# Layer 0's mixer weights: low parts kept in DRAM between the pass over ctx and the pass over x

## The chip, the cores and the metric

One core of one Trainium2 chip runs the whole program. The metric is the device time of one execution in microseconds (us); a time is the median of several runs. The engines are TensorE (PE; its weight loads are PEld), VectorE (DVE), ScalarE (ACT), GpSimd (POOL) and SyncE (SP), which here does nothing but issue DMA transfers. Each engine runs its own instructions in the order of the program and waits where a result or a buffer is not there yet.

## What is computed

Two transformer blocks in float32, on 256 tokens of 1024 features. The first block works on x alone. The second has two layers (`DEPTH_2 = 2`) and two streams, x and ctx, of 256 tokens each. In layer 0 both streams go through the same mixer with the same weights, ctx first, since x attends to the keys, values and states that ctx leaves:

```python
for l in range(DEPTH_2):
    ...
    if last:
        mem = _context_memory(hc, p)
    else:
        yc, mem = _context_mixer(hc, p)
        ...
    x = _post(x, _latent_mixer(_modulate(x, sh1, sc1), mem, cos, sin, p), g1, ln1_g[l], ln1_b[l])
    x = _post(x, _ffn(_modulate(x, sh2, sc2), p), g2, ln2_g[l], ln2_b[l])

def _latent_mixer(h, mem, cos, sin, p):
    proj = h @ p['w_in']
    ...                                   # attention, gated linear attention, convolution of 31 taps
    return _merge(o_att, o_gla, r, glu, gates, p)    # three branches, gated, then w_out
```

In layer 1 the ctx stream needs only its keys, values and states, so only a part of the weights is used twice there.

## The kernel before

**Weights.** All weights come as *units* of 128 x 1024 float32 (512 KB), in the order in which they are used; `program` is run once with a stand-in to record that order (`self.order`), and then again to write the instructions. A product of float32 quality is made of three passes in the faster float32r form: `mm3` multiplies the weight's high part `whi` with the high part of the input, `whi` with the input's low part, and the weight's low part `wlo` with the input's high part. Each pass is 8 products of 128 x 256, so a unit is 24.

**The stream** (`unit` and `load`). When unit n is asked for, `unit` has SP issue the loads of the `raw` tiles up to unit n + 4 (5 `raw` buffers), and `load` splits the units up to n + 2: ACT copies `raw` into `whi` (which rounds it), then DVE or POOL subtracts, `wlo = raw - whi` (3 buffers each). Both instructions of the split stand under `high_priority(offset=75)`. A new `raw` load needs the buffer of five units before, which both instructions of the split must have read; a new `wlo` needs the third pass of the unit three before.

**Who subtracts.** `lo_eng` gives a share of the subtractions to POOL and the rest to DVE by counting them: 3 of 5 in layer 0's mixers (phase `m0t` in `LO`), 1 of 2 in the feed-forwards after them (`f0t`), none in the last one (`f1t`). The count also covers the splits of the branches' outputs (`yl`).

**The mixer** (`mix`) takes one stream through 109 units: keys, values, gates, queries, the convolution's input (`glu`), three branches with their gates (`gb0` to `gb2`, 48 units) and `out` (8 units). In its first part the attention's steps, the gated linear attention's (tiles `gF`, `cum`, `ga`) and the convolution's are woven with the products; the convolution is 248 DVE instructions per stream into the tile `ca`, at low priority (`offset=-1000`). The last two branches and `out` are nearly all products. The program calls `mix` for ctx and then for x.

**Order.** The order of each engine's instructions is made when the kernel is built: a scheduler takes what is written in `program` and moves instructions by their priority. On the chip the order is fixed. SP's queue is such an order too: a transfer that waits holds all that are issued behind it.

Of the kernel before, what the change touches and what calls it, by code (L numbers as in the profile page):

```python
# [18 lines left out]
P = 128  # L19
D = 1024  # L20
T = 256
# [6 lines left out]
# column ranges of the first block's w_in  # L28
# [6 lines left out]
# column ranges of the second block's w_in  # L35
# [11 lines left out]
def _plan():  # L47
    """Order of the weight units: (name, kind, count)."""
    p = [("memk", "F", 8), ("memv", "V", 8), ("lrux", "F", 8), ("lrug", "F", 8),
         ("foxq", "F", 8), ("foxk", "F", 8), ("foxv", "V", 8),  # L50
         ("sbq", "F", 8), ("sbk", "F", 8), ("sbv", "V", 8), ("memq", "F", 8)]
    p += [(f"gb{n}", "F", 16) for n in range(4)]
    p += [("out", "F", 8), ("gu", "F", 2 * FT), ("dn", "D", 24)]
    for l in range(2):
        p += [(f"k{l}", "F", 2), (f"v{l}", "V", 2), (f"kg{l}", "F", 4), (f"vg{l}", "V", 8), (f"glr{l}", "F", 1),
              (f"q{l}", "F", 8), (f"qg{l}", "F", 4), (f"r{l}", "F", 8), (f"glu{l}", "F", 16)]
        p += [(f"gb{n}_{l}", "F", 16) for n in range(3)]
        p += [(f"out{l}", "F", 8), (f"gu{l}", "F", 2 * FT), (f"dn{l}", "D", 24)]
    pos, o = {}, 0
    for name, _, n in p:  # L60
        pos[name] = o
        o += n
    return pos, o
# [4 lines left out]
# columns of the parameter array  # L68
# [18 lines left out]
# those of the first block alone  # L87
# [42 lines left out]
def _pack(x):  # L130
    """Lays the inputs out as the kernel streams them."""
# [160 lines left out]
def weave(*parts):  # L292
    """Interleaves generators: parts are (generator, steps per turn)."""
    live = list(parts)
    while live:
        live = [(g, n) for g, n in live if step(g, n)]


# the share of the weights whose low part GpSimd works out, the vector engine the rest
# [3 lines left out]
class Null:  # L303
    """Stands in for the chip while the order of the weight units is recorded."""
# [17 lines left out]
class Builder:  # L322
    AHEAD = 2

    def __init__(self, tc, a, ctx, order=None):
# [4 lines left out]
        # weight units: their order if known, what is loaded, what is used  # L330
# [13 lines left out]
        # brings in the scalar engine's table for the first norms  # L344
        warm = cp.tile([P, 1], F32, tag="warm", name="warm")
        self.act(warm, self.eps, AF.Sqrt)
        self.mmp = ep(name="mmp", bufs=3, space=bass.MemoryType.PSUM)
# [44 lines left out]
    def phase(self, name, t1=6, t2=6, t4=0):  # L392
        """Opens the pool of the short-lived tiles of a phase: 1, 2 and 4 KB rings."""
# [30 lines left out]
    def unit(self, idx, n=1024):  # L424
        """The next unit of the stream, split; loads run ahead of the use."""
# [10 lines left out]
        while self.n_ready < min(len(self.asked) + self.AHEAD, len(self.order)):  # L436
            self.ready.append(self.load(*self.raws.pop(0)))
# [3 lines left out]
    def load(self, raw, n):  # L441
        hi = self.wp.tile([P, 1024], F32R, tag="whi", name="whi", bufs=3)
        lo = self.wp.tile([P, 1024], F32R, tag="wlo", name="wlo", bufs=3)
        with self.tc.high_priority(offset=75):
            self.split(raw[:, :n], hi[:, :n], lo[:, :n])
        return hi, lo

    def mm3(self, o, w, x, nk, xk, first=True, last=True):
        """o (+)= w.T @ x over nk contraction tiles, in three float32r passes."""
# [10 lines left out]
    def pair(self, name, i, h, n=2):  # L460
        """Feature-major projection onto n feature tiles, from unit i on: [P, n * T] in PSUM."""
# [7 lines left out]
    def half(self, name, i, h, ps=None):  # L469
        """Unit i of a projection, into the first half of a new bank, or the second half of ps."""  # L470
# [8 lines left out]
    def proj_pair(self, name, ft, h):  # L479
        """Two feature tiles from paired units, [P, T] each in PSUM."""  # L480
# [4 lines left out]
    def tok(self, name, c, h):  # L485
        """Token-major projection onto 256 columns: [P, token tile, 256] in PSUM."""
# [13 lines left out]
    def rsqrt(self, ps, w, n):  # L500
        """1/sqrt(ps / n + EPS) on [P, w]."""
# [10 lines left out]
    def token_rsqrt(self, sq, nd, n):  # L512
        """1/sqrt(mean square + EPS) by token, from the squares of heads of nd tiles of features each, [P, T]:
        a column for each head and token tile."""
# [12 lines left out]
    def root(self, ps, w, n):  # L527
        """1/sqrt(ps / n + EPS) by way of the scalar engine."""
# [5 lines left out]
    def total(self, x, fast):  # L534
        """Sum over the features, on every partition; fast: in the fewest steps after the last feature."""
# [37 lines left out]
    def ln_core(self, x, xc, fast=False):  # L573
        """Centres x into xc; returns 1/std."""
# [9 lines left out]
    def post(self, z, g, b, fast=False):  # L584
        """LayerNorm of z with gain and bias, in place; steps: the norm's factor, then one per feature tile."""
# [13 lines left out]
    def attend(self, q, qr, segs, vt, nd, evac):  # L599
        """q: list of [P(d), T] chunks, without the norm's factor, which is qr (a column for each query tile);  # L600
        segs: lists of [P(d), T] key chunks; vt(kt, d): [P(key), P] values."""
# [35 lines left out]
    # ================= first block ======================================  # L637
# [86 lines left out]
    def halve(self, acc, mx):  # L724
        """Splits acc / 2."""
# [4 lines left out]
    def gated_all(self, name, h, y, acc, first, bias):  # L730
        """Steps, one per feature tile: twice sigmoid(gate) * (y @ w) is added to acc. The first two gates come
        ahead of the products of y, which may still be on its way."""
# [42 lines left out]
    def mem_norm(self, ps, out, g):  # L775
        """RMS norm of a head of 256 features (two feature tiles)."""
# [10 lines left out]
    def lru(self, h, y, bp):  # L787
        nc = self.nc
        for f in range(0, KT, 2):
# [13 lines left out]
            # gelu (tanh form) without its factor 1/2  # L803
# [11 lines left out]
    def lru_pair(self, f, xc, ga, y):  # L815
        nc = self.nc
        # nl = -log a = (tanh + 1) * (4 softplus(-lam)); ix = (tanh + 1) * xc = 2 i xc
# [13 lines left out]
        # -expm1(2 log a) = tanh(-log a) * (1 + a^2)  # L831
# [7 lines left out]
        # the scan and ga each carry a factor 2  # L839
# [4 lines left out]
    def fox(self, h, y, bp):  # L844
        nc = self.nc
        # forget gates: cumulative -log sigmoid, [16 heads, T]
# [11 lines left out]
        # -log_sigmoid(z) = ln(1 + exp(-|z|)) - min(z, 0)  # L858
# [19 lines left out]
        # the row that carries -cum_f of the key: where the other head's features are  # L878
# [19 lines left out]
    def fox_head(self, q, k, cm, rows):  # L898
# [4 lines left out]
        # negated masked logits and their minimum  # L903
# [17 lines left out]
    def softplus_abs(self, out, z):  # L921
        """ln(1 + exp(-|z|))"""
# [4 lines left out]
    def av_pair(self, y, ft, v, j, pts):  # L927
        """Two heads' values, side by side in the columns of the array."""
# [28 lines left out]
    def stick_pair(self, y, ft, v, j, qs, k, bp):  # L957
        """Two heads: those of one feature tile."""
# [4 lines left out]
        for half, q in enumerate(qs):  # L963
            z = self.ps("z")
            self.mm(z[:, :T], k[:, :P], q)
            # the bank's first product clears its accumulation bits, so this one overwrites and later ones add
# [5 lines left out]
        # softplus(z), only where key < query  # L972
# [5 lines left out]
        # z minus the suffix sums over keys  # L978
# [14 lines left out]
    # ================= feed-forward =====================================  # L993
    def ffn(self, gu, dn, h, hidden, down, bp):
        """Steps: one per hidden tile, then one per pair of output tiles."""
# [24 lines left out]
    # ================= second block =====================================  # L1020
    def ada(self, l):
        """Modulation vectors of layer l for x (0) and ctx (1), [P, 48] each, with 1 added to the scales;
        and the steps that work them out."""
# [3 lines left out]
    def ada_steps(self, l, out):  # L1027
        """24 steps, four to a group of 1024 features. Their tiles come from self.fp; loads run ahead, up to
        step self.span."""
# [33 lines left out]
    def flush(self):  # L1063
        """Ends the group of modulation vectors whose sums are under way."""
# [25 lines left out]
    def qk_norm(self, ps, out, g):  # L1090
        """RMS norm over the 128 features of [P, 512]."""
# [7 lines left out]
    def rope(self, t):  # L1099
        """t: [P, 2, T], in place."""  # L1100
# [8 lines left out]
    def gla_in(self, l, h, bp, with_q):  # L1109
        """Projections of the gated linear attention; returns their tiles and the steps, one per unit pair."""  # L1110
# [34 lines left out]
    def gates_cum(self, glr, hp):  # L1145
        """Cumulative log gates times 16: [P, dir, head, T], forward and backward, two heads."""
# [23 lines left out]
    def gla_pair(self, l, hp, qk, vg, glr, S, new_S):  # L1170
        """Two heads of one stream; S: states around the sequence, or None; new_S: where to leave the states
        after it, or None; leaves the normed output in qk."""
# [76 lines left out]
    def gla_state(self, hp, qk, vg, cum, S):  # L1249
        """States after the sequence (forward) and before it (backward) of two heads."""  # L1250
# [32 lines left out]
    def modulate(self, x, ada, j, got, pool=None, fast=False):  # L1283
        """The LayerNorm of x with scale j + 1 and shift j of ada, split, left in got. Steps: the norm's factor,
        then, with its tiles, one per feature tile."""
# [17 lines left out]
    def ctx_memory(self, l, h, bp, keep):  # L1303
        """What layer l hands from ctx to x: keys, values and states."""
# [54 lines left out]
    def mix(self, l, h, x, ada, mem, bp, keep, then=None):  # L1359
        """The mixer of one stream, x with its memory, or ctx without: h is its input, x its residual, which  # L1360
        becomes the normed sum. then: steps of the next modulation, which from the second on
        take the place of h.
        Returns what ctx hands to x."""
# [31 lines left out]
        # the sum of the branches takes the place of values and queries  # L1395
# [54 lines left out]
    def layer_ffn(self, l, h, x, ada, bp):  # L1450
        """Steps of the feed-forward of h, added to the residual x."""
# [13 lines left out]
    # ================= the program ======================================  # L1465
    def setup(self):
# [3 lines left out]
        # halved biases for sigmoid(z) = (1 + tanh(z / 2)) / 2  # L1470
# [3 lines left out]
        # 4 softplus(-lam)  # L1474
# [18 lines left out]
        # silu of the conditioning vectors  # L1493
# [8 lines left out]
class Tiles:  # L1502
    """A list of [P, N] tiles, indexed as one [P, k, N] tile."""
# [88 lines left out]
```

## Time and profile before

| | |
|---|---|
| time, median of 3 runs | 3206.67 us (3205.02 to 3207.41) |
| span of the profiled execution, first to last instruction | 3193.8 us |
| median less span | 12.9 us |
| PE busy | 2779.4 us, 87% of the span |
| DVE busy | 2501.7 us, 78% |
| ACT busy | 1469.1 us, 46% |
| POOL busy | 1241.1 us, 39% |
| granted TensorE clock, mean | 0.944 of full speed |
| read from HBM / written | 459.58 MB / 1.05 MB |

The mixer of ctx runs from about 945 to 1426 us of the span, that of x from 1426 to 1931 us (the first product of its first weight to the last of `out`). Shares of the whole span say little here: each mixer has a middle part in which DVE's row is full, and an end in which PE's is. So the profile is read by stretches. "Idle before <- X" in a row means that the engine stood still until X was done. A TensorE clock (PEclk) of 1.00 is 2.4 GHz; the other level is 1.2 GHz, and a mean between is a mixture of the two.

### The profile page before, as it was taken

To read this page: it belongs to the slowest core of one execution; us is meant where nothing else is said; L and a number is where in the kernel's file an instruction comes from. 1 tells how busy PE (TensorE), PEld (TensorE's weight loads), DVE (VectorE), ACT (ScalarE), POOL (GpSimd) and SP (SyncE) were. 2 spreads that over 40 slices of the span, in tenths; PEclk is the share of its full clock that TensorE was granted. 3 is DMA by queue.
4 is the path that set the end of the run, shared out by engine and by line. 5 is a ranking of instruction groups with operands and counts; after the bars stand their busy time and mean duration, and the time that the engine had idled before them with its cause. 6 is when DMAs were issued, how large, how long until landed. Compare 5 with 4: busy or idle time off the path is not lost. (4 is left out here: it accounts for less than half of the span.)

```text
span 3193.8 us, 51920 instructions
## 1 busy us (share of the span) xinstructions
PE 2779.4 (87%) x20768; PEld 2657.8 (83%) x20768; DVE 2501.7 (78%) x3546; ACT 1469.1 (46%) x2189; POOL 1241.1 (39%) x792
## 2 busy tenths in 40 slices
PE   7998889987898878898887798999998888889898
PEld 6897778887898878798787798999897778789798
DVE  7598763779866999877999979878857799985554
ACT  5564456443445434445443354445446543344543
POOL 3243322243323435543435644444543344454000
PEclk9999999989999889999998898999999999999999
DMA  5454323556453232443222445664753323235353
GB/s 201 133 172 165 119 100 126 185 198 217 163 170 119 95 109 89 145 155 103 93 100 87 136 161 184 238 214 169 284 180 101 106 87 103 83 138 179 112 182 109
DMA packets 122035, 464.03 MB, mean 145 GB/s; under 512 B 14140, under 2 KB 14268, under 8 KB 115264
## 3 DMA queue, kind: packets, MB, share of 16 engines
q1 hardware_dynamic: 121104, 460.14, 42.1%
q8 instruction: 163, 2.67, 0.3%
q14 instruction: 80, 0.66, 0.1%
q10 hardware_dynamic: 688, 0.56, 0.1%
HBM read 459.58 MB, written 1.05 MB: 144 GB/s over the span
## 5 line engine op out<-in xcount | busy, mean ns | idle before, releaser
L356 POOL TENSOR_TENSOR wlo<-raw,whi 128x1024 fp32r<-128x1024 f32 (+1 forms) x388 | 1015.9, 2621 | 1254.7 <-ACT whi L353 944.3
L353 ACT ACTIVATE whi<-raw 128x1024 fp32r<-128x1024 f32 (+1 forms) x776 | 805.4, 1045 | 873.6 <-PE mm L366 573.4
L356 DVE TENSOR_TENSOR wlo<-raw,whi 128x1024 fp32r<-128x1024 f32 (+1 forms) x388 | 503.0, 1298 | 253.4 <-ACT whi L353 233.3
L366 PE MATMUL mm<-hh,whi 128*128 128x256 f32 x3776 | 582.7, 296 | 55.7 <-DVE cv L356 25.4
L366 PE MATMUL mm<-hh,wlo 128*128 128x256 f32 x3776 | 568.1, 293 | 55.0 <-DVE wlo L356 53.7
L366 PEld LDWEIGHTS mm<-hh,whi 128*128 128x128 f32 x3776 | 518.2, 200 | 71.4 <-DVE cv L356 28.1
L366 PEld LDWEIGHTS mm<-hh,wlo 128*128 128x128 f32 x3776 | 511.9, 199 | 61.7 <-DVE wlo L356 57.3
L366 PE MATMUL mm<-hl,whi 128*128 128x256 f32 x3776 | 561.4, 291 | 0.0
L366 PEld LDWEIGHTS mm<-hl,whi 128*128 128x128 f32 x3776 | 510.4, 199 | 3.7 <-issue 3.0
L359 DVE SCALAR_TENSOR_TENSOR ca<-yp,pv,ca 128x256 f32<-128x256 f32 x720 | 455.2, 685 | 2.0
L359 DVE SCALAR_TENSOR_TENSOR adacc<-wada,sc,adacc 128x1024 f32<-128x1024 f32 x140 | 232.8, 1679 | 8.4 <-DMA wada<-in_wa 8.1
L366 PE MATMUL mm<-yh,whi 128*128 128x256 f32 x1152 | 177.7, 296 | 18.7 <-ACT yh L353 16.8
L366 PEld LDWEIGHTS mm<-yh,whi 128*128 128x128 f32 x1152 | 159.5, 202 | 23.9 <-ACT yh L353 21.6
L366 PE MATMUL mm<-yh,wlo 128*128 128x256 f32 x1152 | 172.2, 291 | 8.3 <-DVE wlo L356 8.3
L366 PE MATMUL mm<-yl,whi 128*128 128x256 f32 x1152 | 172.6, 292 | 3.8 <-DVE yl L359 3.4
L366 PEld LDWEIGHTS mm<-yh,wlo 128*128 128x128 f32 x1152 | 155.4, 198 | 10.0 <-DVE wlo L356 9.1
L366 PEld LDWEIGHTS mm<-yl,whi 128*128 128x128 f32 x1152 | 156.3, 199 | 5.3 <-DVE yl L359 4.1
L356 POOL TENSOR_TENSOR gF<-cum 128x128 f32<-128x128 f32 x192 | 97.7, 538 | 114.3 <-PE ga L366 80.7
L366 PE MATMUL mm<-hidh,whi 128*128 128x256 f32 x704 | 101.8, 285 | 0.9 <-ACT hidh L353 0.9
L366 PE MATMUL mm<-hidh,wlo 128*128 128x256 f32 x704 | 101.1, 284 | 0.8 <-DVE wlo L356 0.7
L366 PE MATMUL mm<-hidl,whi 128*128 128x256 f32 x704 | 101.2, 285 | 0.0
L356 POOL TENSOR_TENSOR ht<-xt,nr 128x256 f32<-128x256 f32 x4 | 3.3, 829 | 236.1 <-DVE nr L531 218.6
(278 smaller groups left out, 3883.5 us busy)
## 6 DMA issues: line engine op xcount, KB each, us to landing
raw<-in_ws SPq DMA_DIRECT2D x744, 512.0 KB, 3.3
wada<-in_wa SPq DMA_DIRECT2D x48, 1024.0 KB, 5.0
raw<-in_ws SPq DMA_DIRECT2D x32, 384.0 KB, 3.2
memt<-in_tok SPq DMA_DIRECT2D x4, 256.0 KB, 3.9
xt<-in_tok SPq DMA_DIRECT2D x1, 1024.0 KB
ct<-in_tok SPq DMA_DIRECT2D x1, 1024.0 KB, 5.7
wl<-in_wl SPq DMA_DIRECT2D x1, 1024.0 KB
out<-xt SPq DMA_DIRECT2D x4, 256.0 KB, 2.5
```

What stands on the lines that cost most here:

```text
L353: return self.nc.scalar.activation(out, in_, f, **k)
L356: return (eng or self.nc.vector).tensor_tensor(out=out, in0=a, in1=b, op=op)
L359: return self.nc.vector.scalar_tensor_tensor(out=out, in0=a, scalar=s, in1=b, op0=op0, op1=op1)
L366: return self.nc.tensor.matmul(out, lhsT=l, rhs=r, start=start, stop=stop, **k)
```

## The change

In the mixer of ctx, each unit that the program's order has twice, under an index below that of layer 0's feed-forward (`gu0`), is stored after its subtraction: SP writes the `wlo` tile into a DRAM tile of its own, one for each of the 109 units. In the mixer of x, `load` finds the kept tile: SP loads it into `wlo`, ACT makes `whi` from `raw` as before, and no subtraction is issued. The raw units are still loaded for both streams. Comments and texts that explain the functions are removed too; with the added lines, line numbers grow by 2 (`split`, `mm`, `act`) to 10.

```diff
@@ __init__
+        self.dp = ep(name="dp", bufs=1, space=bass.MemoryType.DRAM)
+        self.kept = {}
...
@@ unit
-            self.ready.append(self.load(*self.raws.pop(0)))
+            self.ready.append(self.load(*self.raws.pop(0), *self.order[self.n_ready]))
...
-    def load(self, raw, n):
+    def load(self, raw, n, i, _):
         hi = self.wp.tile([P, 1024], F32R, tag="whi", name="whi", bufs=3)
         lo = self.wp.tile([P, 1024], F32R, tag="wlo", name="wlo", bufs=3)
+        kept = self.kept.pop(i, None)
         with self.tc.high_priority(offset=75):
+            if kept is not None:
+                self.nc.sync.dma_start(lo.bitcast(F32), kept)
+                self.act(hi[:, :n], raw[:, :n])
+                return hi, lo
             self.split(raw[:, :n], hi[:, :n], lo[:, :n])
+        if i < POS["gu0"] and self.order.count((i, n)) > 1:
+            kept = self.kept[i] = self.dp.tile([P, 1024], F32, tag=f"lo{i}", name="lo")
+            self.nc.sync.dma_start(kept, lo.bitcast(F32))
         return hi, lo
```

What moves is seen in SP's order and in DVE's. SP, towards the end of the mixer of ctx (the loads of five units of the branches; `lo` is the tile in DRAM). Before:

```order
L434 DMA raw_13518<-in_ws 128x1024
L434 DMA raw_13548<-in_ws 128x1024
L434 DMA raw_13582<-in_ws 128x1024
L434 DMA raw_13617<-in_ws 128x1024
L434 DMA raw_13647<-in_ws 128x1024
```

The same loads now:

```order
L436 DMA raw_13764<-in_ws 128x1024
L455 DMA lo_13770<-wlo_13767 128x1024
L436 DMA raw_13801<-in_ws 128x1024
L455 DMA lo_13807<-wlo_13804 128x1024
L436 DMA raw_13833<-in_ws 128x1024
L455 DMA lo_13839<-wlo_13836 128x1024
L436 DMA raw_13870<-in_ws 128x1024
```

Between any two raw loads there is now a store, which waits for the subtraction of its unit; the load behind it is that of the unit three later (`raw_13801` belongs to the unit three after that of `lo_13770`).

SP, at the end of the mixer of x (units of the third branch), now; before, this place holds the raw loads alone:

```order
L449 DMA wlo_18720<-lo_13734 128x1024
L436 DMA raw_18656<-in_ws 128x1024
L449 DMA wlo_18754<-lo_13770 128x1024
L436 DMA raw_18687<-in_ws 128x1024
L449 DMA wlo_18789<-lo_13807 128x1024
L436 DMA raw_18717<-in_ws 128x1024
```

Here a load of a kept low part stands ahead of the raw load of its own unit. It waits until PE has done with the `wlo` buffer, which is the end of the unit three before, and the raw load waits behind it.

DVE, in the middle of the mixer of x, where the second pair of heads of the gated linear attention begins. Before:

```order
L359 SCALAR_TENSOR_TENSOR ca<-yp,pv,ca 128x256 x4
L356 TENSOR_TENSOR wlo<-raw,whi 128x1024
L359 SCALAR_TENSOR_TENSOR ca<-yp,pv,ca 128x256 x26
L359 SCALAR_TENSOR_TENSOR ge<-gz,ge 128x512 x2
L356 TENSOR_TENSOR wlo<-raw,whi 128x1024
L1166 SCALAR_TENSOR_TENSOR cum<-ones,ge 128x256 x4
L356 TENSOR_TENSOR gF<-cum 128x128 x4
L356 TENSOR_TENSOR wlo<-raw,whi 128x1024
```

The same place now:

```order
L361 SCALAR_TENSOR_TENSOR ca<-yp,pv,ca 128x256 x35
L361 SCALAR_TENSOR_TENSOR ge<-gz,ge 128x512 x2
L1176 SCALAR_TENSOR_TENSOR cum<-ones,ge 128x256 x4
L358 TENSOR_TENSOR gF<-cum 128x128 x4
L361 SCALAR_TENSOR_TENSOR ca<-yp,pv,ca 128x256 x5
```

The subtractions are gone from DVE's order, and the instructions of the convolution have closed up ahead of `ge`.

## Rows read from the trace of the kernel before

**Rows 1.** Stretches, first mixer then second: engine busy (instructions), PEclk, DMA share, GB/s

```profile
945.00:1426.00 481.00, 412.24 (x3040) 396.07 (x3039) 411.81 (x654) 213.18 (x310) 222.19 (x181) 0.93 0.36 121
1426.00:1931.00 505.00, 426.33 (x3100) 408.58 (x3100) 449.36 (x702) 226.72 (x329) 243.60 (x153) 0.93 0.34 114
```

**Rows 2.** Start, middle and end of the mixer of x (PE, PEld, DVE, ACT, POOL)

```profile
1426.00:1480.00 54.00, 42.52 (x285) 40.15 (x285) 47.27 (x65) 27.56 (x42) 21.59 (x10) 0.84 0.36 118
1480.00:1830.00 350.00, 288.35 (x2059) 274.82 (x2058) 324.90 (x541) 149.46 (x211) 173.58 (x121) 0.93 0.29 101
1830.00:1931.00 101.00, 95.46 (x761) 93.61 (x760) 77.19 (x98) 49.70 (x79) 48.43 (x22) 0.98 0.47 159
```

**Rows 3.** What PE waited for from 1480 to 1830: us in total, times, longest

```profile
PE mm L366 <- DVE wlo L356: 23.3, 4, 10.0
PE ga L366 <- DVE gF L356: 14.5, 5, 4.0
PE lg L366 <- DVE nt L359: 9.0, 2, 4.7
PE pt L626 <- DVE pr L363: 9.0, 6, 2.0
```

**Rows 4.** Instructions on `wlo` alone, middle and whole mixer of x: PE, PEld, DVE, POOL

```profile
1480.00:1830.00 350.00, 83.94 (x536) 73.69 (x536) 32.80 (x26) 119.56 (x42) 0.93 0.29 101
...
sum 505.00, PE 134.55 PEld 119.79 DVE 53.20 POOL 181.63; mean PE 44.85 PEld 39.93 DVE 17.73 POOL 60.54
```

**Rows 5.** DVE groups from 1480 to 1830: busy us, mean ns | idle before

```profile
L359 DVE SCALAR_TENSOR_TENSOR ca<-yp,pv,ca 128x256 f32<-128x256 f32 x240 | 152.6, 689 | 0.6
L356 DVE TENSOR_TENSOR wlo<-raw,whi 128x1024 fp32r<-128x1024 f32 x26 | 32.8, 1262 | 3.8 <-ACT whi L353 3.2 <-PE mm L366 0.4
```

**Rows 6.** The tile `ca`: instructions, duration ns min/median/max

```profile
L359 DVE SCALAR_TENSOR_TENSOR ca<-yp,pv,ca x720: 458/479/2686, 1031.6 to 2829.3; 128x256 f32<-128x256 f32 x180
```

**Rows 7.** DVE in time, 1694 to 1700: start us, us taken

```profile
1694.48 0.87 DVE L359 SCALAR_TENSOR_TENSOR ca<-yp,pv,ca 128x256 f32<-128x256 f32 x2
...
1696.74 3.33 DVE L359 SCALAR_TENSOR_TENSOR ca<-yp,pv,ca 128x256 f32<-128x256 f32 x3
```

**Rows 8.** POOL in time, the same stretch

```profile
1694.88 3.83 POOL L356 TENSOR_TENSOR wlo<-raw,whi 128x1024 fp32r<-128x1024 f32 x1 [2.73 <-ACT whi L353]
```

**Rows 9.** PE in time, one unit at the end of the mixer of x

```profile
1886.21 1.12 PE L366 MATMUL mm<-hh,whi 128*128 128x256 f32 x8
...
1889.10 1.12 PE L366 MATMUL mm<-yh,whi 128*128 128x256 f32 x8
```

**Rows 10.** Stretches of the mixer of ctx: its start and the last branches

```profile
945.00:1000.00 55.00, 53.14 (x413) 50.60 (x412) 29.46 (x52) 25.93 (x38) 22.83 (x26) 1.00 0.50 159
1300.00:1426.00 126.00, 115.92 (x911) 113.33 (x912) 100.52 (x117) 61.12 (x93) 64.15 (x33) 0.97 0.48 159
```

**Rows 11.** One us each while raw loads are in flight (last: DMA share, GB/s)

```profile
1140.00:1141.00 1.00, 0.31 (x1) 0.31 (x2) 1.00 (x4) 0.00 (x0) 0.00 (x0) 0.50 1.00 393
1141.00:1142.00 1.00, 1.00 (x3) 0.82 (x3) 1.00 (x4) 0.00 (x0) 0.00 (x0) 0.50 1.02 324
```

**Rows 12.** The busiest stretch of DMA, in layer 0's feed-forward

```profile
2260.00:2310.00 50.00, 45.25 (x368) 43.55 (x367) 40.59 (x40) 21.32 (x33) 23.85 (x12) 0.97 0.80 306
```

**Rows 13.** DMA issues from 2260 to 2310: KB each, median us to landing

```profile
raw<-in_ws SPq DMA_DIRECT2D x15, 512.0 KB, 7.0
```

**Rows 14.** DMA issues of the whole execution: KB each, median us to landing

```profile
raw<-in_ws SPq DMA_DIRECT2D x744, 512.0 KB, 3.3
wada<-in_wa SPq DMA_DIRECT2D x48, 1024.0 KB, 5.0
...
out<-xt SPq DMA_DIRECT2D x4, 256.0 KB, 2.5
```

**Rows 15.** ACT and POOL in time, 1383 to 1388

```profile
1383.93 1.06 ACT L353 ACTIVATE whi<-raw 128x1024 fp32r<-128x1024 f32 x1 [1.58 <-PE mm L366]
...
1385.06 2.40 POOL L356 TENSOR_TENSOR wlo<-raw,whi 128x1024 fp32r<-128x1024 f32 x1 [3.35 <-ACT whi L353]
```

## The prediction

> **What bounds the kernel now.** I read the stretches of both mixers first [rows 1], then the mixer of x cut in three [rows 2]. In its middle, 350 us long, DVE is busy for 324.9 us and PE for only 288.35; in its end, 101 us, PE is busy for 95.46 and DVE has a quarter of its time free. So DVE sets the pace in the middle and PE at the end. The reader should take one step more for PE: its busy time contains the slow clock. At full speed the middle's products would take 288.35 x 0.93 = 268 us. The 350 us are then 268 of products, 20 of half clock, and 350 - 288 = 62 in which PE stands.
>
> What PE waits for in the middle comes next [rows 3]: DVE, for the low parts of the weights (23.3 us) and for results that stand in DVE's queue behind other work (`ga`, `lg` and `pt`, 14.5 + 9.0 + 9.0 us). Then what fills DVE [rows 5]: 26 subtractions of 1262 ns, and 240 steps of the convolution at a mean of 689 ns, where their median over the run is 479 and their minimum 458 [rows 6]. The time lines show why the mean is high: two steps of `ca` take 0.87 us together while POOL is idle; three begun at 1696.74, while POOL subtracts from 1694.88 to 1698.71, take 3.33 [rows 7, 8]. A step that reads two tiles in SBUF stands until POOL's instruction ends. So a low part costs DVE time even where POOL works it out.
>
> **The change part by part.** *Subtractions taken out of the mixer of x.* DVE loses 53.2 us of its own there and POOL 181.6; in the middle 32.8 (26 instructions) and 119.6 (42) [rows 4]. With POOL's gone the 240 steps of `ca` should run at their median: 240 x (0.689 - 0.479) = 50 us. DVE's 325 us in the middle become 325 - 33 - 50 = 242 or less, since other steps with two inputs are held in the same way. Against the 278 us that PE needs it is no longer the bound.
>
> What PE then still waits: the 23.3 us for `wlo` go, since a load of a low part needs no engine. Of the other 39 us the two ends are that none goes (they are chains, from PE over DVE back to PE) and that all goes. The nearest row is the end of the same mixer [rows 2], where DVE is busy for 76% and PE stands 5.5 of 101 us, 5.5%; of some 290 us that is 16. Of the 20 us of slow clock I take half: the clock reads 0.93 where PE stands often and 0.98 at the end, where it doesn't. The middle becomes 268 + 10 + 16 = 294, a gain of 56. The start (54 us, DVE 47.27) shares some of it; I put 4, between 0 and the 11 us in which PE stands there. The end is PE's already: gain 0.
>
> *Copies by ACT, order of PE.* ACT does the same work; the products are the same. Free.
>
> *109 stores in the mixer of ctx.* They need no engine, and move 109 x 0.524 MB. What they touch is SP's queue: a store waits for its subtraction, and the raw load of the unit three later stands behind it. In the middle of that mixer the products are slow (DVE is the bound) and this is hidden. Where PE sets the pace, a unit takes 2.88 us (1886.21 to 1889.10, [rows 9]): at the start of ctx's mixer and in its last branches [rows 10], 159 GB/s x (55 + 126) us / 0.524 MB = 55 units. There the loop is: subtraction of unit k-3 done, load of k, copy by ACT 1.06 us, subtraction 2.40 on POOL [rows 15]. It has three units, 8.64 us, so it holds while the load lands within 8.64 - 3.46 = 5.2 us.
>
> *109 loads in the mixer of x.* They are hidden in its middle, where units come slowly. At its end (159 GB/s x 101 us [rows 2] = 31 units) the load of `wlo` waits for PE to leave the unit three before, and the raw load waits behind it: landing and copy must fit into two units, 5.76 us, so the landing into 4.7.
>
> Can such landings be had? Loads of 512 KB land in 3.3 us, those of 1024 KB, which is a raw unit and a low part together, in 5.0 [rows 14]. Loads in flight moved 393 and 324 GB/s in a microsecond [rows 11], and the busiest stretch kept 306 for 50 us [rows 12]. A unit now needs 1.049 MB. I take 350 GB/s, between the two peaks: 3.0 us a unit, 0.12 more than PE's 2.88, and 0.12 x (55 + 31) = **10 us lost**. Bounds: none at 364 GB/s or above; at 306, 3.43 us a unit, 47 us. Waits of PE at the ends could bring the clock down too; the 0.97 of ctx's branches [rows 10] leaves little to say on this, and it is in the upper bound.
>
> The microsecond at 393 GB/s is the trace's answer on the ceiling. The Trainium skill ("DMA: Bandwidth & Descriptors", Specifications) puts what HBM gives one core at about 358 GB/s, below what these rows reached; an estimate by it would be 2.93 us a unit and 4 us lost instead of 10.
>
> *Sum.* -56 - 4 + 10 = -50 us. The profiled execution spans 3193.8 us and becomes 3144; the median of the runs, 3206.67, lies 12.9 us above the span, and I keep that: **3157 us**.
>
> **Rivals.** *Landing paces the dense units (slower).* If a load next to a store and another load lands late, SP's queue, and no longer PE, sets the pace of the 86 dense units. For it: 15 raw loads between 2260 and 2310 took a median of 7.0 us [rows 13]; a store of half the size takes 2.5 us to land with nothing beside it [rows 14], and a new subtraction into a `wlo` must await its store. Against: in that stretch several loads stood in flight at once, while here one waits for the next. With a landing of L us the loss is 55 x (L - 5.2) / 3 + 31 x (L - 4.7) / 3; it eats the 60 us of the gain at L = 7.1. At 7.0 and one more unit in the way (0.524 MB at 306 GB/s, 1.7 us) L is 8.7, the loss 106: -60 + 106 = +46, **3253 us**.
>
> What speaks for long landings of stores in particular is a sentence of the Trainium skill ("DMA: Bandwidth & Descriptors", Anatomy of one DMA): the fixed part of a transfer is mostly the confirmation that its last byte has landed, and this is longest where the target is HBM. The page tells it of another issue path, and the 2.5 us for 256 KB here don't show it.
>
> *PE alone is the bound (faster still).* All waits in the middle but a few go, and the clock follows as in the end: 268 / 0.98 = 274, a gain of 76; the start gains 10; DMA costs nothing. -86, **3121 us**. For it: nearly all of PE's waits name DVE. Against: the chains of attention and of `gF` have steps of their own.
>
> *The waits are chains.* Only the 23.3 us for `wlo` go; `ga`, `lg`, `pt` and the clock stay, since DVE's order, not its load, sets them. -23 + 10 = -13, **3194 us**. Against: they last up to 4.7 us each, longer than any single step of DVE that PE would have to await.
>
> That the change doesn't do what it says is excluded by SP's order: 109 stores and 109 loads stand there, and the subtractions are gone.
>
> **How the numbers follow.** Forecast 0.60, PE alone 0.17, slow landings 0.12, chains 0.11. 0.2%, about 6.4 us, is what a measurement of this kernel can tell from no change. Faster by more than that: the forecast but for the worst of its DMA bound, PE alone, and most of the chains' case, 0.84. Slower: slow landings beyond L = 7.3, 0.10. The same: what lies between, 0.06. The range goes from 3112 (9 us below PE alone) to 3204 (the forecast with the DMA bound of 47 is 3194; with a middle that gains 46 instead of 56 it is 3204), and leaves out the slow landings and a little below.
>
> **What would show it.** In the profile after: the mixer of x at about 445 us instead of 505, its middle at 294; the mean of `ca` there near 480 ns, but still near 690 in the mixer of ctx; DVE some 80 us less busy in the middle; no wait of PE for a subtraction, and what is left named `ga`, `lg` and `pt`. In the dense stretches, units of 3.0 us, raw loads landing in about 5, and PE's waits of a few tenths of a us on copies or on the loads of `wlo`. If the units there take 3.4 us or more, the landing term was too small; if the middle keeps 320 us with DVE at 240, the waits were chains; if `ca` stays at 690 ns, POOL's subtractions weren't what held it.

## The result, and the profile after

| | before | after |
|---|---|---|
| time, median of 4 runs each | 3205.85 us (3199.85 to 3207.41) | 3129.64 us (3124.27 to 3138.93) |
| ratio, 95% interval | | 0.977 (0.9749 to 0.9792) |
| span of the profiled execution | 3193.8 us | 3137.1 us |
| DVE busy | 2501.7 us | 2356.0 us |
| POOL busy | 1241.1 us | 1054.3 us |
| PE busy | 2779.4 us | 2771.5 us |
| read from HBM / written | 459.58 / 1.05 MB | 516.73 / 58.20 MB |

The kernel is 76 us faster by the medians; 50 were forecast, and the time lies inside the range. It is 27 us below the forecast of 3157 and 9 us above the rival "PE alone", 3121. The two spans differ by 57 us only: the span of before, 3193.8 us, is that of an execution shorter than any of its four timed ones, and that of after was the longest of its four (3138.93 us). So the stages are compared by what they do, and the rest of the execution is looked at by itself further down.

To compare stages, the mixers are cut at the same units in every kernel (first product of a unit to the first of a later one), not at the same times. Mixer of ctx: the first 12 units, the next 66, the last 31. Mixer of x: the first 11, the next 66, the last 32. In us:

| kernel | ctx start | ctx middle | ctx end | x start | x middle | x end | both mixers | ahead of them | behind them |
|---|---|---|---|---|---|---|---|---|---|
| before | 44.1 | 333.6 | 99.9 | 54.7 | 347.0 | 102.8 | 982.2 | 932.1 | 1239.9 |
| after | 44.2 | 331.6 | 110.7 | 49.3 | 275.3 | 106.1 | 917.1 | 930.8 | 1250.2 |

The mixer of x got 74 us shorter, that of ctx 9 longer. The same stretches as windows (length, then PE, PEld, DVE, ACT, POOL busy with their instructions, PEclk, DMA share, GB/s): first the end of ctx before, then, in the kernel after, the end of ctx and start, middle and end of x.

```profile
1326.50:1426.40 99.90, 94.36 (x752) 92.51 (x751) 76.35 (x96) 48.83 (x77) 48.34 (x22) 0.98 0.48 159
```

```profile
1322.70:1433.40 110.70, 98.85 (x752) 96.08 (x750) 76.51 (x105) 54.19 (x84) 48.53 (x23) 0.94 0.83 295
1433.40:1482.70 49.30, 44.03 (x310) 40.86 (x311) 31.86 (x63) 29.42 (x46) 3.31 (x3) 0.97 0.83 300
1482.70:1758.00 275.30, 265.99 (x2013) 255.55 (x2012) 216.72 (x504) 143.31 (x200) 48.69 (x80) 0.99 0.68 247
1758.00:1864.10 106.10, 98.38 (x776) 95.36 (x775) 46.11 (x94) 55.06 (x87) 5.56 (x6) 0.98 0.87 315
```

The middle of x answers to [rows 2]: DVE was busy for 325 of 350 us there, now for 217 of 275; PE stands for 9 us where it stood for 62, and the granted clock rose from 0.93 to 0.99. What PE still waits for in the middle (us in total, times, longest) answers to [rows 3]; `wlo`, `nt` and `pr` are gone or down to 1 us:

```profile
PE ga L368 <- DVE gF L358: 5.8, 6, 2.7
PE av L368 <- ACT ptsb L355: 1.1, 1, 1.1
PE lg L368 <- DVE nt L361: 1.0, 1, 1.0
```

The convolution, which answers to [rows 5], in the middle of x, and below it in the mixer of ctx of the same execution (DVE groups: busy us, mean ns | idle before):

```profile
L361 DVE SCALAR_TENSOR_TENSOR ca<-yp,pv,ca 128x256 f32<-128x256 f32 x240 | 103.7, 479 | 0.9
```

```profile
L361 DVE SCALAR_TENSOR_TENSOR ca<-yp,pv,ca 128x256 f32<-128x256 f32 x240 | 153.2, 688 | 0.7
```

The same 240 steps take 479 ns each in x, where POOL no longer subtracts, and 688 in ctx, where it still does.

The price is seen at the end of ctx. What PE and ACT wait for there: first the longest item of each before, from 1326.5 to 1426.4, then after, from 1322.7 to 1433.4:

```profile
PE st L366 <- DVE sq L356: 2.3, 2, 2.2
```

```profile
ACT whi L353 <- PE mm L366: 18.1, 11, 2.3
```

```profile
PE st L368 <- DVE sq L358: 4.7, 1, 4.7
PE mm L368 <- DVE yl L361: 2.8, 1, 2.8
PE mm L368 <- ACT whi L355: 1.3, 2, 0.9
```

```profile
ACT whi L355 <- DMA raw<-in_ws: 18.2, 12, 3.6
```

ACT's copies, which waited for PE before, now wait for the raw loads, 18.2 us in twelve waits. PE itself waits for a copy for 1.3 us only; its longer waits are for work of DVE (`sq`, `yl`). DMA issues in the same stretch (KB each, median us to landing), to be held against the 3.3 of [rows 14]:

```profile
lo<-wlo SPq DMA_DIRECT2D x31, 512.0 KB, 3.8
raw<-in_ws SPq DMA_DIRECT2D x30, 512.0 KB, 5.0
```

The same from the page, over the whole execution:

```profile
raw<-in_ws SPq DMA_DIRECT2D x744, 512.0 KB, 3.8
lo<-wlo SPq DMA_DIRECT2D x109, 512.0 KB, 3.3
wlo<-lo SPq DMA_DIRECT2D x109, 512.0 KB, 3.7
```

### The profile page after: what moved, and what is told of

It is laid out like the page before. It is cut to its first block, busy times and chain, and to the rows that moved or that the text cites. A ratio compares the mean times of both kernels' runs of the same rounds, so it can differ in the third digit from the quotient of the medians.

```text
span 3137.1 us, 52191 instructions
## 1 busy us (share of the span) xinstructions
PE 2771.5 (88%) x20768; PEld 2652.9 (85%) x20768; DVE 2356.0 (75%) x3502; ACT 1470.0 (47%) x2189; POOL 1054.3 (34%) x727
## 3 DMA queue, kind: packets, MB, share of 16 engines
HBM read 516.73 MB, written 58.20 MB: 183 GB/s over the span
## 5 line engine op out<-in xcount | busy, mean ns | idle before, releaser
L358 POOL TENSOR_TENSOR wlo<-raw,whi 128x1024 fp32r<-128x1024 f32 (+1 forms) x323 | 838.9, 2601 | 1153.0 <-ACT whi L355 822.6
L358 DVE TENSOR_TENSOR wlo<-raw,whi 128x1024 fp32r<-128x1024 f32 (+1 forms) x344 | 456.9, 1330 | 264.5 <-ACT whi L355 241.7
L361 DVE SCALAR_TENSOR_TENSOR ca<-yp,pv,ca 128x256 f32<-128x256 f32 x720 | 410.0, 619 | 2.3
L368 PE MATMUL mm<-yh,whi 128*128 128x256 f32 x1152 | 180.4, 297 | 25.2 <-ACT yh L355 18.2
L368 PEld LDWEIGHTS mm<-hidl,whi 128*128 128x128 f32 x704 | 93.1, 194 | 2.9 <-DVE hidl L358 2.9
```

What stands on the lines that cost most here:

```text
L358: return (eng or self.nc.vector).tensor_tensor(out=out, in0=a, in1=b, op=op)
L361: return self.nc.vector.scalar_tensor_tensor(out=out, in0=a, scalar=s, in1=b, op0=op0, op1=op1)
L368: return self.nc.tensor.matmul(out, lhsT=l, rhs=r, start=start, stop=stop, **k)
```

## The experiments

Three questions were open: what held DVE in the mixer of x, what the traffic costs and why, and where the rest of the 76 us is. The kept loads without the stores were to be measured too (load_only), but that kernel gave no result, so the loads have no price of their own here. This is the table above for the kernels that were run, with the ratio to the kernel before.

| kernel | ratio (95%) | ctx start | ctx middle | ctx end | x start | x middle | x end | both mixers | behind them |
|---|---|---|---|---|---|---|---|---|---|
| same_count | 0.9768 (0.9748 to 0.9788) | 44.1 | 333.0 | 109.8 | 49.4 | 275.3 | 105.3 | 916.9 | 1236.5 |
| pool_share | 0.9725 (0.9708 to 0.9742) | 44.1 | 332.7 | 99.9 | 44.0 | 280.3 | 97.3 | 898.3 | 1247.5 |
| dve_share | 0.9952 (0.9936 to 0.9968) | 44.1 | 333.4 | 99.9 | 62.9 | 327.1 | 102.8 | 970.2 | 1248.1 |
| store_only | 1.0036 (1.0019 to 1.0052) | 44.3 | 332.8 | 110.1 | 55.5 | 349.4 | 104.2 | 996.3 | 1249.4 |
| store_hi | 1.0032 (1.0021 to 1.0043) | 41.4 | 331.5 | 110.7 | 58.2 | 349.3 | 104.3 | 995.4 | 1249.3 |
| late_store | 0.9776 (0.976 to 0.9792) | 44.1 | 331.3 | 107.3 | 54.0 | 275.0 | 101.7 | 913.4 | 1245.9 |
| act_both | 0.9779 (0.9764 to 0.9795) | 40.4 | 340.6 | 112.5 | 42.8 | 282.6 | 101.7 | 920.6 | 1233.0 |
| keep_mid | 0.9811 (0.979 to 0.9832) | 44.1 | 333.0 | 103.8 | 53.9 | 280.0 | 103.7 | 918.5 | 1248.7 |
| share45 | 0.9714 (0.9693 to 0.9736) | 44.1 | 333.0 | 99.9 | 43.5 | 282.2 | 98.5 | 901.2 | 1238.8 |
| store_twice | 1.0032 (1.0015 to 1.0049) | 46.1 | 374.3 | 137.4 | 59.0 | 275.0 | 106.2 | 998.0 | 1248.0 |

**The count, and what lies behind the mixers.** In the changed kernel the units kept no longer advance the count that shares the subtractions, so later units change hands between POOL and DVE.

```diff
                 self.nc.sync.dma_start(lo.bitcast(F32), kept)
+                self.n_lo += 1
```

> The changed kernel, but a kept unit still advances the count that shares the subtractions between POOL and DVE, so that behind the mixer of x every engine has the instructions of the kernel before in the same order. In the profiled pair, what follows the mixer of x took 1252 us with the change and 1242 before. Theory A (the shifted count, which gives other units to POOL, costs those 10 us): the part behind the mixer of x is back at 1242 us and the time is about 3120. Theory B (the 10 us are what one execution differs from another): the time stays within 5 us of the changed kernel, some 3125 to 3135.

Median 3124.47 us, ratio 0.9768 against 0.977: no difference that can be told. The stretch behind the mixers came back to 1236.5 us, as theory A said, but that doesn't show A: behind the mixers the other kernels of the table have the instructions of the kernel before in the same order, but for a few at the first cut, and take 1233.0 to 1249.4 us. A difference of 14 us between two executions is within that spread. In one part of it, the last 75 units, the changed kernel has that order too; it is the first row, same_count the second:

```profile
2860.80:3114.30 253.50, 237.29 (x1825) 231.49 (x1824) 127.25 (x166) 108.24 (x153) 13.45 (x7) 0.95 0.41 142
```

```profile
2849.50:3097.10 247.60, 231.38 (x1825) 226.69 (x1824) 126.87 (x166) 108.15 (x153) 13.44 (x7) 0.98 0.42 145
```

DVE and ACT are as busy in both; PE is busy 6 us longer at a granted clock of 0.95 instead of 0.98. So 6 of the 14 us are what one execution differs from another by its clock. In the part just ahead of it, where the changed kernel's order is its own, it takes 428.8 us (from 2432.0 to 2860.8), and the other kernels 419.0 to 423.4; whether the count costs something there stays open. All later kernels keep the count of before (`same_count` is their base).

**What held DVE.** One half of the relief each: in pool_share 65 low parts are kept, in the pattern of 3 in 5 that is POOL's share, and DVE subtracts the other 44; in dve_share the 44 are kept, and POOL subtracts the 65.

```diff
+            if 337 <= self.n_ready < 446:
+                self.n_lo += 1
+                self.split(raw[:, :n], hi[:, :n], lo[:, :n], self.nc.vector)
+                return hi, lo
...
-        if i < POS["gu0"] and self.order.count((i, n)) > 1:
+        if i < POS["gu0"] and self.order.count((i, n)) > 1 and (self.n_ready + 109) * 3 // 5 != (self.n_ready + 108) * 3 // 5:
```

In dve_share the engine is `self.nc.gpsimd` and the last comparison is `==`.

> Kept are the low parts of 65 units, those whose number falls on POOL in a pattern of 3 in 5; the other 44 are subtracted by DVE in the mixer of x, so POOL subtracts none there. Theory A (POOL's subtractions hold DVE's steps with two inputs in SBUF): steps of the convolution at 480 ns in the middle of x, DVE's busy time there 325 - 50 or more, some 250 to 275 us, the middle 285 to 300 us instead of 347. Rival (the convolution's mean of 689 ns has another cause, and only DVE's own 33 us of subtractions count): middle at 335 us or more.

> The counterpart: kept are the 44 other units, and POOL subtracts 65 in the mixer of x, DVE none. Theory A: the convolution stays near 690 ns, DVE's busy time in the middle falls by its own 33 us only, to about 290, and the middle takes 310 to 320 us. Rival (DVE's own subtractions are the whole matter): middle at 290 us or less, convolution at 480 ns.

The middle of x in pool_share, its window and two of its DVE groups:

```profile
1467.00:1747.30 280.30, 270.97 (x2036) 259.77 (x2035) 253.16 (x541) 146.71 (x206) 49.82 (x79) 0.99 0.56 198
```

```profile
L361 DVE SCALAR_TENSOR_TENSOR ca<-yp,pv,ca 128x256 f32<-128x256 f32 x240 | 107.3, 500 | 0.7
L358 DVE TENSOR_TENSOR wlo<-raw,whi 128x1024 fp32r<-128x1024 f32 x26 | 32.2, 1238 | 4.1 <-ACT whi L355 3.9
```

And in dve_share:

```profile
1482.50:1809.60 327.10, 279.36 (x2013) 266.99 (x2012) 278.62 (x508) 143.90 (x200) 164.36 (x118) 0.94 0.41 146
```

```profile
L361 DVE SCALAR_TENSOR_TENSOR ca<-yp,pv,ca 128x256 f32<-128x256 f32 x240 | 144.7, 652 | 0.9
```

With POOL's subtractions gone and DVE's 26 still there, the convolution runs at 500 ns and the middle takes 280 us, 67 of the 72 us gained and 5 us better than theory A. With DVE's gone and POOL's there, it runs at 652 and the middle takes 327, a gain of 20, where 310 to 320 us were expected. Each half takes load off the same engine, so the two gains are not to be added. What bound the middle of x was POOL's hold on DVE far more than DVE's own subtractions.

pool_share is also faster than the changed kernel as a whole: 3115.3 us. It loses nothing at the end of ctx, and both ends of x are shorter.

**What the traffic costs.** First the stores alone, the mixer of x subtracting as before; then the same number of bytes without SP's queue and without a wait for the subtraction, by storing the high part from ACT.

```diff
-        kept = self.kept.pop(i, None)
+        kept = None
...
-            self.nc.sync.dma_start(kept, lo.bitcast(F32))
+            self.nc.scalar.dma_start(kept, hi.bitcast(F32))
```

The second pair of lines is in store_hi alone; both store each unit of ctx once.

> The 109 stores stay in the mixer of ctx, and the mixer of x subtracts as before and loads nothing kept. Theory A (the stores cost what the traces of the pair show, 8 us of the mixer of ctx, in its dense units): mixer of ctx 485 us instead of 478, time 3206 + 8 = 3214. Rival (the stores are free, and the 8 us are those of one execution): 3206, mixer of ctx 478. Rival (stores pace the dense units, as in the case of slow landings): 3206 + 50 or more.

> No low part is kept; the mixer of x subtracts as before. In the mixer of ctx ACT issues a store of each unit's high part right behind its copy: the 109 stores have the same bytes as with the change, but SP's queue holds raw loads alone and no store waits for a subtraction. Theory A (bytes: the dense end of ctx loses because DMA has 1 MiB to move per unit): end of ctx 106 to 110 us as with store_only, time 3208 to 3214. Rival (the order of SP's queue, a load behind a store behind a subtraction): end of ctx 100 to 102 us, time within 4 us of the kernel before.

store_only took 3213.7 us and store_hi 3211.22, 0.4 and 0.3% above the kernel before; in both the end of ctx takes 110 us instead of 99.9, and its start nothing more. So the stores alone, without the kept loads, bring the loss at the end of ctx, also where SP's queue holds raw loads alone. That it is their bytes isn't shown. The window of the end of ctx in store_hi, to be held against the 159 GB/s before, and the longest wait of ACT there:

```profile
1320.40:1431.10 110.70, 96.08 (x751) 94.01 (x751) 78.02 (x100) 52.25 (x83) 47.23 (x22) 0.95 0.78 279
```

```profile
ACT whi L355 <- DMA lo<-whi: 28.3, 15, 4.0
```

In store_hi no copy waits for a raw load: a copy waits for a `whi` buffer, which is free only when its store has landed. That is another wait than in the changed kernel, and the same 110 us.

Two kernels that keep everything, with the queue eased. late_store issues each store one unit later; act_both has stores and kept loads issued by ACT.

```diff
+        due, self.due = self.due, None
+        if due is not None:
+            self.nc.sync.dma_start(*due)
...
-            self.nc.sync.dma_start(kept, lo.bitcast(F32))
+            self.due = kept, lo.bitcast(F32)
```

> same_count with each store issued one unit later: in the dense end of the mixer of ctx the raw load of a unit stands behind the store of the unit four before instead of three. The bytes are the same. Theory A (the 10 us that the end of ctx's mixer lost come from SP's queue: a raw load is issued only when a subtraction three units back is done, and its landing of 5.0 us then comes too late for ACT): the end of ctx takes 101 to 104 us instead of 110, the time is about 7 us under same_count, 3117. Rival (1 MiB a unit is more than DMA moves in 2.88 us): the end stays at 110 us, the time at 3124.

> late_store, but the stores and the loads of kept low parts are issued by ACT, behind the copy of their unit, so that SP's queue holds raw loads alone, as in the kernel before. Theory A (the queue is what costs): end of ctx 100 to 103 us, end of x 102 to 104 instead of 105, time 3112 to 3118. Rival (ACT, which now waits for subtractions and for PE's third pass with everything of its own behind it, makes the copies late): end of ctx or of x above 110 us, time 3130 or more. Rival (bandwidth): both ends as in same_count, 3124.

Neither did what theory A said. late_store took 2.5 us off the end of ctx where 6 to 9 were expected; act_both made it 112.5 and the middle of ctx 8 us longer, with a start of x that is 7 us shorter; neither is faster than same_count. The end of ctx in late_store:

```profile
1323.50:1430.80 107.30, 96.69 (x752) 94.19 (x750) 76.20 (x100) 48.90 (x78) 47.94 (x22) 0.95 0.78 278
```

No wait of ACT for a raw load shows there any more, and 7 of the 10 us of loss remain. So late raw loads, which the changed kernel shows, can't be the whole of it.

Then fewer bytes. keep_mid keeps only the 67 units that the mixers use in their middles (the condition of the store gets `and 239 <= self.n_ready < 306`); share45 keeps 4 in 5 all through (`and self.n_ready % 5`, DVE subtracting the fifth).

> Low parts are kept for 67 of the 109 units alone, the 12th to the 78th, which the two mixers use in their middles; the dense units at the start and the end of both have the traffic of before and subtract. Theory A (the gain is made in the middle of x, and the dense units only lose by the traffic): of the 72 us of the middle nearly all stay, the 8 us in ctx and the 3 us at the end of x are not lost, the 5 us at the start of x are not gained: about 6 us faster than same_count, some 3115 to 3125. Rival (the subtractions also hold up the dense units, so that to be rid of them pays for the traffic): slower than same_count by 5 us or more.

> As pool_share, but kept are 4 units in 5 instead of 3; DVE subtracts the fifth in the mixer of x and POOL none. Theory A (what the ends of the mixers lose grows with the bytes): end of ctx 102 to 105 us (pool_share 99.9, all kept 109.8), end of x 99 to 102 (97.3 and 105.3), middle of x 276 to 280, time some 3117 to 3122. Rival (there is no loss up to nearly 1 MiB a unit, and more kept is better): below pool_share's 3115.

keep_mid was not the faster one: its stages sum to 918.5 us against the 916.9 of same_count. It lost 6 us less in ctx, but the start of x, which subtracts again, went back to 53.9, and the middle took 280.0, though one subtraction (1.6 us of POOL) is all that is left in it; why is not shown. Its median, 3138.37, is 14 us above that of same_count, as its rival said; but 12 of these are in the stretch behind the mixers, which has the same instructions in both, so it stays open what the change itself does. share45 has the lowest time of all, 3111.35 us, which is not to be told from pool_share's 3115.3. Its end of ctx, and the longest wait of ACT there:

```profile
1325.10:1425.00 99.90, 94.36 (x752) 92.52 (x751) 76.35 (x96) 48.70 (x77) 48.30 (x22) 0.98 0.80 286
```

```profile
ACT whi L355 <- PE mm L368: 16.5, 10, 2.3
```

It moves 286 GB/s, more than the 279 of store_hi, but takes the 99.9 us of the kernel before, and ACT waits for PE again, though a raw load lands in 5.0 us as in the changed kernel. So neither 286 GB/s nor this landing time costs anything by itself.

The traces show a rival that no run tests: the order of the instructions. The scheduler may place the instructions of DVE and ACT anew when stores are added. In share45, pool_share and dve_share both engines have the order of the kernel before at the end of ctx, instruction for instruction (96 of DVE in each window), and all three take 99.9 us. Every kernel that loses there has another order (98 to 105 of DVE in the window, 91 in store_twice); keep_mid is one of them and takes 103.8, although it stores nothing in that stretch and moves 170 GB/s. Whether one unit in five without a store, or the order that came with it, saves the 10 us stays open.

Last, the cost doubled: each low part stored twice.

```diff
             self.nc.sync.dma_start(kept, lo.bitcast(F32))
+            self.nc.sync.dma_start(self.dp.tile([P, 1024], F32, tag=f"lp{i}", name="lp"), lo.bitcast(F32))
```

> same_count with each low part stored twice in the mixer of ctx, into two tiles of DRAM: 1.57 MB a unit instead of 1.05 in ctx, all else alike. Theory A (bytes set the pace of the dense end of ctx, at the 293 GB/s that it moved with one store): 31 units x 1.573 MB / 293 GB/s = 166 us for the end of ctx instead of 110, and its start, 12 units in 44 us now, becomes 64; time near 3200, the gain all but gone. Rival (the order of the queue and the landing behind one store was the cost): end of ctx 115 to 125 us, time 3130 to 3140.

The end of ctx, then a longer window across its beginning; below, the landings from 1330 to 1460:

```profile
1367.40:1504.80 137.40, 108.82 (x748) 102.11 (x748) 60.87 (x91) 51.07 (x79) 51.25 (x23) 0.89 0.90 338
```

```profile
1320.00:1475.00 155.00, 120.33 (x840) 112.43 (x839) 70.69 (x86) 56.56 (x87) 61.60 (x31) 0.91 0.96 365
```

```profile
raw<-in_ws SPq DMA_DIRECT2D x31, 512.0 KB, 7.0
lo<-wlo SPq DMA_DIRECT2D x30, 512.0 KB, 5.1
lp<-wlo SPq DMA_DIRECT2D x30, 512.0 KB, 6.2
```

3211.86 us: the whole gain is gone. The end of ctx took 137 us, between the two expectations: DMA moved 338 GB/s there and not 293. The start of ctx took 46.1, not 64. The middle of ctx, which had hidden one store, lost 41 us, and the start of x 10. DMA can move more than the 295 GB/s of the changed kernel: 365 over 155 us, at a DMA share of 0.96 where the end of ctx in the changed kernel has 0.83. With the landing of a raw load at 7.0 us, the kernel is near where the rival of the prediction put its break-even, 7.1; that is chance, since half of the loss lies in the middle of ctx, where that rival had none.

## Why the prediction was right, and where its terms were off

- *POOL's hold on DVE*: right. Steps of the convolution at 479 ns, forecast 480; the two half kernels show that it is this, and not DVE's own subtractions, that made the middle long.
- *The whole*: 65 us by stages where the sum said 50, and 76 by the medians. The gain in x came out as in the rival "PE alone"; that rival's free DMA did not.
- *The middle of x*: the mechanism was right, the size too small, 72 us gained instead of 56. Two terms were mis-sized. The remaining waits of PE were taken from the end of x (5.5% of the time at a DVE that is 76% busy, 16 us); they are 9.3 us, 3.4%, at a DVE that is 79% busy: the waits at the end of x were a few single ones (`sq` 2.2, `gt` 1.7, `yh` 0.7, `yl` 0.6 us), which say little about the middle. And of the 20 us of slow clock all but some 3 went (266 us at 0.99), not half. It came out at the rival "PE alone", 274. The rival of the chains is refuted: with the chains still there, `ga`, `lg` and `pt` wait 5.8, 1.9 and 0.2 us in all, where they waited 14.5, 9.0 and 9.9.
- *The start of x*: 5.4 us gained, forecast 4.
- *The end of x*: 3.3 us lost, forecast 3.7.
- *ctx*: 8.8 us lost, forecast 6.6, but not as it was worked out. Its start loses nothing, its middle gains 2.0 and its end loses 10.8. Of these, PE's busy time is 4.5 us (98.85 us at a clock of 0.94, against 94.36 at 0.98) and its waits 6.3 us. The clock had been left to the upper bound.
- *The 10 us of DMA*: 12 were lost, and that the sizes agree is luck. The sum took 2.88 us for a unit, which is one unit without a wait; before, the 12 units at the start of ctx took 44.1 us, 3.7 each, and the 31 at its end 99.9, 3.2 each. At 350 GB/s, 3.0 us a unit, neither would have lost anything on the average. Nor is it the landing: at the start of ctx raw loads landed in 5.6 us, above the 5.2 that the loop allowed, and 0.1 us was lost; at the end they landed in 5.0. What makes the end of ctx lose is open, as said above. At the end of x the wait is the forecast one: ACT's copies wait 33.3 us for raw loads there, and PE 6.8 us for the copies.
- *350 GB/s*: not contradicted, but not the right figure to work with. At the end of x 315 GB/s were moved, at the end of ctx 295, with a loss in each; the end of x in late_store moved 327 and took 101.7 us, no more than before. The highest of a long stretch is the 365 of store_twice, over 155 us. The Trainium skill ("DMA: Bandwidth & Descriptors", Specifications) gives about 358 for one core; this stretch came above it, and the measurement decides.
- *Slow landings*: 5.0 us was forecast for raw loads among stores and measured, below the 7.1 at which the gain would have gone. Over the whole execution a store landed in 3.3 us and a kept load in 3.7: stores issued by SP were not the slow kind. Issued by ACT, in store_hi, they took 5.9 us where raw loads took 4.5 (1323 to 1426).
- *12.9 us around the span*: wrong in what it is. In all runs with a span beside them the time is 1.8 to 1.9 us above it (3138.93 and 3137.1); the other 11 of the 12.9 were the distance of a short execution to the median.

By stages the change gains 65 us (982.2 to 917.1). The medians say 76. The stretches ahead of the mixers and behind them, which the change doesn't touch but for the count, take 926 to 932 and 1233 to 1250 us in the kernels of the table; the 11 us lie within that, and nothing closer was found.

## What to carry to other kernels

Work that is given to POOL is not free for DVE: price it by what it does to DVE's instructions with two inputs in SBUF, by the mean against the median of one such group. To load a result again instead of working it out again paid where an engine was the bound, and cost where PE was; here to keep a part of it beat to keep all. A change that adds transfers can also change the order of the engines' instructions: compare that order before a loss is put down to the bytes. When two profiles are compared, compare first a stretch that the change doesn't touch.

## What the runs showed that was not expected

- Keeping 4 units in 5 (0.9714) or 3 in 5 (0.9725) beats keeping all (0.9768): at 286 GB/s, with the order of the kernel before, the end of ctx loses nothing; at 293, with another order, it loses 10 us.
- DMA held 365 GB/s over 155 us in store_twice, while the changed kernel lost time at 295.
- In pool_share the end of x is faster than in the kernel before, 97.3 us against 102.8, although it moves 274 GB/s instead of 159: PE stands for 2 us there instead of 5.5. POOL is all but idle there (5.5 us), which may leave DVE's last steps free; the order differs too, and nothing separates the two.
- The same instructions in the same order took 247.5 to 253.5 us at the end of the kernel; the shortest had a granted clock of 0.98, the longest 0.95.
